# A hybrid decoder layer on one core: subtractions and convolution taps moved from VectorE to GpSimd and ScalarE, and other weight buffers in one stage

## The chip, the core and the metric

The kernel runs on one core of a Trainium2 chip. A core has TensorE (PE, matrix products out of SBUF into PSUM), VectorE (DVE), ScalarE (ACT), GpSimd (POOL) and SyncE (SP, which issues most DMA transfers). Each engine works through its own queue in order, and waits on semaphores for the others. SBUF has 128 partitions; a "128x512" operation works on 512 elements in each. The metric is the device time of one execution in microseconds (us), lower is better. The granted TensorE clock of a stretch is given as a share of full speed.

## What is computed

One decoder layer, for 512 tokens of width 2048 in fp32. One input projection feeds two branches, whose gated outputs are summed, projected and added to the input (the reference, cut):

```python
h = rms_norm(x, norm_g)
proj = jnp.einsum('bsd,dn->bsn', h, w_in)
(q_a, k_a, v_a, o_a, i_a, f_a, z_a, c_q, c_kv, k_r, z_b, g_a, g_b) = jnp.split(proj, offsets, axis=-1)

qk_a = jax.nn.silu(causal_depthwise_conv(jnp.concatenate([q_a, k_a], axis=-1), conv_w))
q_a, k_a = jnp.split(qk_a, 2, axis=-1)
h_a = mlstm_chunkwise(q_a, k_a, v_a, i_a + gate_bias[:H_A], f_a + gate_bias[H_A:])
h_a = rms_norm(h_a, mlstm_norm_g)
y_a = jnp.einsum('bsc,cd->bsd', jax.nn.sigmoid(o_a) * h_a * jax.nn.silu(z_a), w_a)
...
o_b = causal_attention(q_b, k_b, v_b)
y_b = jnp.einsum('bsc,cd->bsd', o_b * jax.nn.silu(z_b), w_b)

y = jax.nn.sigmoid(g_a) * y_a + jax.nn.sigmoid(g_b) * y_b
return x + jnp.einsum('bsd,de->bse', y, w_out)
```

The convolution has four taps along the tokens, for each channel by itself:

```python
xp = jnp.pad(x, ((0, 0), (CONV_K - 1, 0), (0, 0)))
out = xp[:, CONV_K - 1:] * w[CONV_K - 1]
for j in range(CONV_K - 1):
    out = out + xp[:, j:j + s_len] * w[j]
```

## The kernel before

**Numbers in two parts.** Each fp32 operand of a product is split into a high and a low part: ACT casts it (`split`, L105), DVE subtracts the cast from the source (L106). A product is then three matmuls, high by high, high by low and low by high (`mm3`, L113 to L115, and in the Strassen stage L506 to L508).

**Stages.** The order of the work on each engine comes from a scheduler in the tile framework, which keeps data and buffer dependencies; the code gives the rough order by `weave` (a main generator, with a filler put between its steps) and by `later` (a list of small pieces, one of which `run_later` takes after each step of a product).

1. To about 124 us: the input is transposed and normalized, and the latents and gates are projected (`load_c`, `proj_tok`). Beside it, `build(j)` makes for each of eight pairs of row blocks the operands of the Strassen products: `normal` (L304) scales `f` by the norm, `parts` splits it, `combine` (L323 to L326) makes four sums of 256 elements, `split_sums` splits these.
2. To about 905 us: ten jobs of a one-level Strassen scheme (`strassen`). A job makes 1024 columns of the input projection with seven products p = 0 to 6 in place of eight, and each product has four steps j, 28 steps of 12 matmuls in a job. `prep` loads a block of weights (`rx`, 5 buffers, and `rr`, a ring of 8) and, for p = 1, 2, 4 and 6, subtracts blocks (`minus`, L462). `part` splits the result into `wh` (3 buffers) and `wl` (2 buffers). `mult` multiplies. `finish` takes the results out of PSUM. In the code `prep` runs two steps ahead of `mult`, `part` one step.
3. To about 1387 us: eight pairs of attention heads (`pair_attn`), with the projections for later pairs as filler. The outputs `go` are stored to `gb` (L857) by SP.
4. To about 1690 us: the mLSTM branch. `conv_qk` projects two blocks of 128 channels of q or k, takes each through the convolution and silu, and splits it into `qkT`. In `evac` ACT copies the projection from PSUM into `xp`, behind three zeros (L969, L970); DVE multiplies by the last tap (L980) and adds the other three taps one by one (L977). ACT's tanh (L985) and three more operations make silu and the split. `pair_qk` of the next two heads, and then the first block of `out_b`, are the filler for `heads`. There, POOL makes the causal mask of each tile (`affine_select`, L1037) and the reciprocal root for the norm (`rsqrt`, L120 to L124).
5. To the end: `out_b(1..3)`, the product with `w_a`, and the one with `w_out`.

**Weights of stages 3 to 5.** `load_w` takes 256 KB at a time: `raw` from SP (4 buffers, L137), `whi` (NB_W = 3 buffers) and `wlo` (NB_L = 2). All come from one pool, `wp`, from the attention on to the end. `reload` in stage 4 brings back the attention's outputs and splits them into `g`; it takes nothing but `raw` from that pool. `out_b(d)` also loads `u`, 1 MB of gates.

**The pools.** `open_pool` and `close_pool` give and take space of SBUF. A tile of a pool that is opened in the place of a closed one waits for the tiles that lay there.

Of the kernel before, what the change touches and what calls it, by code (L numbers as in the profile page):

```python
# [19 lines left out]
P = 128  # L20
# [17 lines left out]
NB_X, NB_RING, NB_HI, NB_LO = 5, 8, 3, 2  # L38

# [5 lines left out]
def hybrid_kernel(  # L45
# [81 lines left out]
    wpool = [None]  # L127

    def load_w(src, col, width, kn, first=0):
        per = max(1, 512 // width)  # L130
        hi = lo = None
        for i in range(kn):
            k = (i + first) % kn
            if k % per == 0:
# [6 lines left out]
                hi = wp.tile([P, per, width], F32R, tag="whi", name=nm("whi"), bufs=NB_W)  # L141
                lo = wp.tile([P, per, width], F32R, tag="wlo", name=nm("wlo"), bufs=NB_L)
# [157 lines left out]
    def build(j):  # L300
        f = whole[j]

        def normal():
            V.tensor_tensor(f, f, rB.unsqueeze(1).broadcast_to([P, 2, S]), ALU.mult)  # L304
# [15 lines left out]
        def combine():  # L320
            a, b = tmp(512, "s12"), tmp(512, "s34")
            s1, s2, s3, s4 = a[:, 0:256], a[:, 256:512], b[:, 0:256], b[:, 256:512]
            V.tensor_tensor(s1, f[:, 0, 256:512], f[:, 1, 256:512], ALU.add)  # L323
            V.tensor_tensor(s3, f[:, 0, 0:256], f[:, 0, 256:512], ALU.subtract)
            V.tensor_tensor(s2, s1, f[:, 0, 0:256], ALU.subtract)
            V.tensor_tensor(s4, f[:, 1, 0:256], s2, ALU.subtract)  # L326
            sums.extend((a, b))
# [112 lines left out]
    def strassen(jobs, comb):  # L440
# [15 lines left out]
        def prep(c, p, j):  # L456
# [4 lines left out]
            def minus(dst, a, b):  # L461
                V.tensor_tensor(dst, a, b, ALU.subtract)  # L462
# [497 lines left out]
    close_pool("bpa")  # L960
    big_pool[:] = [(open_pool("bph"), NB_HEAD)]


    def conv_qk(p, base, blk, res):

        def evac(s, ps):
            k = blk + 2 * p + s
            xp = tmp(516, "xp")
            G.memset(xp[:, 0:3], 0.0)  # L969
            A.copy(xp[:, 3:515], ps)  # L970
            o = big([P, 2, S], F32R, "qkT")
            cv = tmp(512, "cv")
            th = tmp(512, "th")

            def taps(j0, j1):
                for j in range(j0, j1):
                    V.scalar_tensor_tensor(cv, xp[:, j:j + S], cw[:, k, j:j + 1], cv, ALU.mult, ALU.add)  # L977
# [273 lines left out]
```

## Time and profile before

| | |
|---|---|
| runs | 2171.72, 2172.4 and 3008.73 us, median 2172.4 us |
| profiled execution | 2176.62 us, of it 2174.9 us in the span of the profile |
| granted TensorE clock, mean | 0.991 |
| busy: PE, DVE, ACT, POOL | 2121.5, 1395.4, 983.0, 173.2 us |

"Busy" is the time in which an engine executes; a matmul is shown from its start to its modelled end, and overlaps the next. A row of a group of instructions reads: line of the code, engine, operation, output <- inputs by the names in the code (numbers left out), partitions x elements, count; then busy us in total, mean ns of one, and the idle time of the engine just before them, with what ended it. A row of the timeline begins with start and duration in us.

### The profile page before, as it was taken

How to read it: one execution, taken by the hardware profiler on the slowest of the kernel's cores; microseconds unless marked ns; L12 is line 12 of the kernel's file. 1: busy time of each engine (PE TensorE's matmuls, PEld its weight loads, DVE VectorE, ACT ScalarE, POOL GpSimd, SP SyncE). 2: the span in 40 equal slices, each digit the busy share in tenths (PEclk: the TensorE clock that was granted, in tenths of full speed). 3: DMA queues.
4: the chain of work that ended last, by engine and by line, in shares of the span. 5: the costliest groups of instructions: out<-in, count | busy, mean ns of one | idle time of the engine just before them, and what ended most of it. 6: DMA issues, size and time to landing. Idle time of an engine off the chain costs nothing. (4 is left out here: it accounts for less than half of the span.)

```text
span 2174.9 us, 28907 instructions
## 1 busy us (share of the span) xinstructions
PE 2121.5 (98%) x10200; PEld 1787.8 (82%) x10200; DVE 1395.4 (64%) x2260; ACT 983.0 (45%) x2025; POOL 173.2 (8%) x306
## 2 busy tenths in 40 slices
PE   8999999999999999899999999999989999999999
PEld 8878888888888888688888888877867888888889
DVE  5877788887778788656666677766565334444333
ACT  7544444444444544445555556454445223222221
POOL 0000000000000000222222222011111000000000
PEclk9999999999999999999999999999999999999999
DMA  6645424633642462632222222464544425332443
GB/s 171 166 166 184 149 90 149 184 108 105 185 149 90 149 204 92 215 89 75 83 77 80 81 80 73 155 190 144 159 134 157 136 97 160 126 131 92 136 131 117
DMA packets 205314, 286.02 MB, mean 132 GB/s; under 512 B 31216, under 2 KB 111472, under 8 KB 204144
## 3 DMA queue, kind: packets, MB, share of 16 engines
q1 hardware_dynamic: 189040, 256.90, 38.9%
q10 hardware_dynamic: 16128, 27.27, 3.6%
q8 instruction: 80, 1.31, 0.3%
q14 instruction: 66, 0.54, 0.1%
HBM read 240.07 MB, written 44.04 MB: 131 GB/s over the span
## 5 line engine op out<-in xcount | busy, mean ns | idle before, releaser
L106 DVE TENSOR_TENSOR wlo<-raw,whi 128x512 fp32r<-128x512 f32 (+3 forms) x432 | 284.3, 661 | 383.5 <-PE acc L114 252.3
L105 ACT CAST whi<-raw 128x512 fp32r<-128x512 f32 (+3 forms) x432 | 259.1, 600 | 526.8 <-PE acc L115 338.0
L106 DVE TENSOR_TENSOR wl<-rx,wh 128x1024 fp32r<-128x1024 f32 x160 | 196.5, 1228 | 114.7 <-PE aux L507 64.7
L105 ACT CAST wh<-rx 128x1024 fp32r<-128x1024 f32 x160 | 168.9, 1055 | 177.9 <-PE acc L508 109.0
L113 PE MATMUL acc<-whi,g 128*128 128x512 f32 x512 | 201.5, 396 | 5.9 <-ACT g L105 5.9
L115 PE MATMUL acc<-whi,g 128*128 128x512 f32 x512 | 199.7, 393 | 1.8 <-DVE g L106 1.8
L114 PE MATMUL acc<-wlo,g 128*128 128x512 f32 x512 | 200.6, 392 | 0.0
L105 ACT CAST wh<-rr 128x1024 fp32r<-128x1024 f32 x120 | 126.4, 1053 | 160.7 <-PE aux L508 88.1
L106 DVE TENSOR_TENSOR wl<-rr,wh 128x1024 fp32r<-128x1024 f32 x120 | 146.3, 1219 | 27.6 <-PE aux L507 14.6
L506 PE MATMUL acc<-wh,sh 128*128 128x512 f32 x400 | 155.6, 389 | 0.0
L507 PE MATMUL acc<-wl,sh 128*128 128x512 f32 x400 | 155.6, 389 | 0.0
L508 PE MATMUL acc<-wh,sl 128*128 128x512 f32 x400 | 155.6, 389 | 0.0
L113 PEld LDWEIGHTS acc<-whi,g 128*128 128x128 f32 x512 | 96.8, 189 | 25.7 <-ACT g L105 6.5
L115 PEld LDWEIGHTS acc<-whi,g 128*128 128x128 f32 x512 | 96.9, 190 | 22.2 <-DVE g L106 2.2
L114 PEld LDWEIGHTS acc<-wlo,g 128*128 128x128 f32 x512 | 96.9, 189 | 20.3 <-DVE wlo L106 0.8
L115 PE MATMUL acc<-h8h,wlo 128*128 128x512 f32 x256 | 102.8, 406 | 10.3 <-DVE wlo L106 10.3
L113 PE MATMUL acc<-whi,y 128*128 128x512 f32 (+1 forms) x320 | 111.1, 348 | 0.0
L115 PE MATMUL acc<-whi,y 128*128 128x512 f32 (+1 forms) x320 | 111.0, 347 | 0.0
L114 PE MATMUL acc<-wlo,y 128*128 128x512 f32 (+1 forms) x320 | 111.0, 347 | 0.0
L113 PE MATMUL acc<-h8h,whi 128*128 128x512 f32 x256 | 103.6, 405 | 2.3 <-ACT whi L105 2.3
L114 PE MATMUL acc<-h8l,whi 128*128 128x512 f32 x256 | 102.5, 400 | 0.0
L113 PE MATMUL acc<-ht,whi 128*128 128x512 f32 x256 | 101.2, 395 | 0.0
(357 smaller groups left out, 5052.6 us busy)
## 6 DMA issues: line engine op xcount, KB each, us to landing
rr<-in_w_in SPq DMA_DIRECT2D x120, 512.0 KB, 4.6
raw<-in_w_in SPq DMA_DIRECT2D x128, 256.0 KB, 2.8
rx<-in_w_in SPq DMA_DIRECT2D x40, 512.0 KB, 5.0
raw<-in_w_b SPq DMA_DIRECT2D x64, 256.0 KB, 3.1
raw<-in_w_a SPq DMA_DIRECT2D x64, 256.0 KB, 3.2
raw<-in_w_out SPq DMA_DIRECT2D x64, 256.0 KB, 3.0
raw<-in_w_ukv SPq DMA_DIRECT2D x32, 256.0 KB, 2.8
raw<-in_w_uq SPq DMA_DIRECT2D x32, 192.0 KB, 2.4
```

The source lines that it names most:

```text
L105: A.copy(dst_hi, src)
L106: V.tensor_tensor(dst_lo, src, f32(dst_hi), ALU.subtract)
L113: PE.matmul(ps, lh, rh, start=start, stop=False)
L114: PE.matmul(ps, lh, rl, start=False, stop=False)
L115: PE.matmul(ps, ll, rh, start=False, stop=stop)
L506: PE.matmul(out[i], lh[:, tok], hi[:, n, :], start=first, stop=False, skip_group_check=cont)
L507: PE.matmul(out[i], lh[:, tok], lo[:, n, :], start=False, stop=False, skip_group_check=cont)
L508: PE.matmul(out[i], ll[:, tok], hi[:, n, :], start=False, stop=k == H8 - 1, skip_group_check=cont)
```

## The change

`normal` and `combine` in `build`, and `minus` in `prep`, are issued to GpSimd (`G`) in place of VectorE (`V`). In `conv_qk`, ACT takes the projection out of PSUM four times, each time scaled by one tap, and GpSimd adds three of these copies, shifted by 1, 2 and 3 tokens, to the fourth; `xp` and its zeros are gone. After the attention the pool `wp` is closed and `wph` opened, with six buffers for `whi` and six for `wlo`; after the mLSTM stage `wph` is closed and `wp` opened again with three and two. The pool of `u` is now two pools, `up0` (for `out_b(0)`) and `up1`.

```diff
 NB_X, NB_RING, NB_HI, NB_LO = 5, 8, 3, 2
+NB_W2, NB_L2 = 6, 6
...
-    wpool = [None]
+    wpool = [None, NB_W, NB_L]
...
-                hi = wp.tile([P, per, width], F32R, tag="whi", name=nm("whi"), bufs=NB_W)
-                lo = wp.tile([P, per, width], F32R, tag="wlo", name=nm("wlo"), bufs=NB_L)
+                hi = wp.tile([P, per, width], F32R, tag="whi", name=nm("whi"), bufs=wpool[1])
+                lo = wp.tile([P, per, width], F32R, tag="wlo", name=nm("wlo"), bufs=wpool[2])
...
         def normal():
-            V.tensor_tensor(f, f, rB.unsqueeze(1).broadcast_to([P, 2, S]), ALU.mult)
+            G.tensor_tensor(f, f, rB.unsqueeze(1).broadcast_to([P, 2, S]), ALU.mult)
...
-            V.tensor_tensor(s1, f[:, 0, 256:512], f[:, 1, 256:512], ALU.add)
-            V.tensor_tensor(s3, f[:, 0, 0:256], f[:, 0, 256:512], ALU.subtract)
-            V.tensor_tensor(s2, s1, f[:, 0, 0:256], ALU.subtract)
-            V.tensor_tensor(s4, f[:, 1, 0:256], s2, ALU.subtract)
+            G.tensor_tensor(s1, f[:, 0, 256:512], f[:, 1, 256:512], ALU.add)
+            G.tensor_tensor(s3, f[:, 0, 0:256], f[:, 0, 256:512], ALU.subtract)
+            G.tensor_tensor(s2, s1, f[:, 0, 0:256], ALU.subtract)
+            G.tensor_tensor(s4, f[:, 1, 0:256], s2, ALU.subtract)
...
             def minus(dst, a, b):
-                V.tensor_tensor(dst, a, b, ALU.subtract)
+                G.tensor_tensor(dst, a, b, ALU.subtract)
...
     close_pool("bpb")
     close_pool("bpa")
+    close_pool("wp")
+    wpool[:] = open_pool("wph"), NB_W2, NB_L2
     big_pool[:] = [(open_pool("bph"), NB_HEAD)]
...
-            xp = tmp(516, "xp")
-            G.memset(xp[:, 0:3], 0.0)
-            A.copy(xp[:, 3:515], ps)
+            cv = tmp(512, "cv")
+            A.activation(cv, ps, AF.Copy, scale=cw[:, k, 3:4])
+            for d in range(1, 4):
+                th = tmp(512, "th")
+                A.activation(th, ps, AF.Copy, scale=cw[:, k, 3 - d:4 - d])
+                G.tensor_tensor(cv[:, d:], cv[:, d:], th[:, :S - d], ALU.add)
             o = big([P, 2, S], F32R, "qkT")
...
-            def taps(j0, j1):
-                for j in range(j0, j1):
-                    V.scalar_tensor_tensor(cv, xp[:, j:j + S], cw[:, k, j:j + 1], cv, ALU.mult, ALU.add)
...
-                V.tensor_scalar(cv, xp[:, 3:515], cw[:, k, 3:4], None, ALU.mult)
...
-            later.extend((first, second, third, fourth))
+            later.extend((lambda: None, silu, lambda: split(o[:, 0, :], o[:, 1, :], cv)))
...
     drain(filler)
     close_pool("bph")
+    close_pool("wph")
+    wpool[:] = open_pool("wp"), NB_W, NB_L
     g2p = open_pool("g2p")
+    ups.append(open_pool("up1", "right"))
```

**The products' stage, first job.** DVE before, from the first subtractions of product 1 on. `rx` and `rr` are blocks of weights, the number tells one buffer's tile from another, `wl` is a low part, and the rows of L106 are splits:

```order
L462 TENSOR_TENSOR rx_1606<-rr_1670,rx_1606 128x1024
L106 TENSOR_TENSOR wl_1674<-rx_1646,wh_1673 128x1024
L462 TENSOR_TENSOR rx_1608<-rr_1695,rx_1608 128x1024
L462 TENSOR_TENSOR rx_1614<-rr_1715,rx_1614 128x1024
L106 TENSOR_TENSOR wl_1699<-rx_1606,wh_1698 128x1024
L462 TENSOR_TENSOR rx_1646<-rr_1737,rx_1646 128x1024
L106 TENSOR_TENSOR wl_1719<-rx_1608,wh_1718 128x1024
L462 TENSOR_TENSOR rx_1606<-rr_1757,rx_1606 128x1024
L462 TENSOR_TENSOR rx_1608<-rr_1776,rx_1608 128x1024
L106 TENSOR_TENSOR wl_1741<-rx_1614,wh_1740 128x1024
```

POOL in the changed kernel, the subtractions of the same job (line 463 now), from the last sum over the input (L327) on:

```order
L327 TENSOR_TENSOR s_321_1665<-hn_347,s_320_1664 128x256
L463 TENSOR_TENSOR rx_1606<-rr_1670,rx_1606 128x1024
L463 TENSOR_TENSOR rx_1608<-rr_1695,rx_1608 128x1024
L463 TENSOR_TENSOR rx_1614<-rr_1715,rx_1614 128x1024
L463 TENSOR_TENSOR rx_1646<-rr_1737,rx_1646 128x1024
L463 TENSOR_TENSOR rx_1606<-rr_1757,rx_1606 128x1024
L463 TENSOR_TENSOR rx_1608<-rr_1776,rx_1608 128x1024
L463 TENSOR_TENSOR rx_1614<-rr_1796,rx_1614 128x1024
L463 TENSOR_TENSOR rx_1646<-rr_1818,rx_1646 128x1024
L463 TENSOR_TENSOR rr_1757<-rr_1757,rr_1670 128x1024
L463 TENSOR_TENSOR rr_1776<-rr_1776,rr_1695 128x1024
L463 TENSOR_TENSOR rx_1606<-rx_1606,rr_1982 128x1024
```

Before, the subtractions stood between the splits on one queue. Now they stand one behind the other on POOL, product 6 (`rx<-rx,rr`) mixed with product 4 (`rr<-rr,rr`), and DVE has the splits alone.

**From the attention to the mLSTM stage, SP.** The stores of `go` and the loads of weights; `raw` from `in_w_in`, 128x2x256, are the weights of `conv_qk(0)`. Before:

```order
L137 DMA raw_12102<-in_w_ukv 128x512
L137 DMA raw_12120<-in_w_ukv 128x512
L137 DMA raw_12595<-in_w_in 128x2x256
L137 DMA raw_12613<-in_w_in 128x2x256
L137 DMA raw_12631<-in_w_in 128x2x256
L137 DMA raw_12649<-in_w_in 128x2x256
L137 DMA raw_12667<-in_w_in 128x2x256
L137 DMA raw_12685<-in_w_in 128x2x256
L857 DMA gb_7332<-go_12240 128x512
L137 DMA raw_12703<-in_w_in 128x2x256
```

In the changed kernel:

```order
L138 DMA raw_12120<-in_w_ukv 128x512
L858 DMA gb_7332<-go_12240 128x512
L858 DMA gb_7332<-go_12316 128x512
L858 DMA gb_7333<-go_12509 128x512
L1109 DMA u_14945<-ggb_1580 128x2048
L858 DMA gb_7333<-go_12585 128x512
L138 DMA raw_12599<-in_w_in 128x2x256
L138 DMA raw_12617<-in_w_in 128x2x256
L138 DMA raw_12635<-in_w_in 128x2x256
```

The weights of `conv_qk(0)` stood ahead of the last four stores; now they stand behind all of them, and behind the load of `u`.

**The same place on PE.** `ptb` and `vl` belong to the last tile of the attention, `acc` of `whi` and `h8h` to `conv_qk(0)`. Before, in the middle of the last pair of heads:

```order
L811 MATMUL aux_12166<-krl_11862,qst_11860 128x256
L835 MATMUL aux_12203<-ident,pr_12097 128x128 x4
L113 MATMUL acc_12593<-h8h_827,whi_12597 128x512
L114 MATMUL acc_12593<-h8l_828,whi_12597 128x512
L115 MATMUL acc_12593<-h8h_827,wlo_12598 128x512
L113 MATMUL acc_12594<-h8h_827,whi_12597 128x512
L114 MATMUL acc_12594<-h8l_828,whi_12597 128x512
```

In the changed kernel, at the end of that pair:

```order
L115 MATMUL aux_12572<-ptb_12514,vh_12040 128x256
L116 MATMUL aux_12572<-ptb_12514,vl_12041 128x256
L114 MATMUL acc_12597<-h8h_827,whi_12601 128x512
L115 MATMUL acc_12597<-h8l_828,whi_12601 128x512
L116 MATMUL acc_12597<-h8h_827,wlo_12602 128x512
```

The projection of `conv_qk(0)` stood between the tiles of the last pair; now its first matmul stands behind the last one of the attention.

More of the change, by code (lines that the diff above doesn't have):

```diff
@@ L967, in evac, with silu @@
             k = blk + 2 * p + s
-            xp = tmp(516, "xp")
-            G.memset(xp[:, 0:3], 0.0)
-            A.copy(xp[:, 3:515], ps)
-            o = big([P, 2, S], F32R, "qkT")
-            cv = tmp(512, "cv")
-            th = tmp(512, "th")
-            def taps(j0, j1):
-                for j in range(j0, j1):
-                    V.scalar_tensor_tensor(cv, xp[:, j:j + S], cw[:, k, j:j + 1], cv, ALU.mult, ALU.add)
-            def first():
-                V.tensor_scalar(cv, xp[:, 3:515], cw[:, k, 3:4], None, ALU.mult)
-                taps(0, 1)
-            def second():
-                taps(1, 3)
+            cv = tmp(512, "cv")
[4 more added lines that the diff above has]
+                G.tensor_tensor(cv[:, d:], cv[:, d:], th[:, :S - d], ALU.add)
+            o = big([P, 2, S], F32R, "qkT")
+            def silu():
+                th = tmp(512, "th")
                 A.activation(th, cv, AF.Tanh, scale=0.5)
-            def third():
                 V.scalar_tensor_tensor(cv, th, 1.0, cv, ALU.add, ALU.mult)
-                A.copy(o[:, 0, :], cv)
-            def fourth():
-                V.tensor_tensor(o[:, 1, :], cv, f32(o[:, 0, :]), ALU.subtract)
-            later.extend((first, second, third, fourth))
+            later.extend((lambda: None, silu, lambda: split(o[:, 0, :], o[:, 1, :], cv)))
             res.append(o)
@@ L1113, in lazily @@
         return get
-    u_t = []
+    u_t, ups = [], []
     def out_b(d):
-        u = up.tile([P, T, 512], F32, tag=f"u{d}", name=f"u{d}")
+        u = ups[-1].tile([P, T, 512], F32, tag=f"u{d}", name=f"u{d}")
         SP.dma_start(u, gb_g[d])
@@ L1160, in hybrid_kernel @@
                 gp = open_pool("gp", "right")
-                up = open_pool("up", "right")
+                ups.append(open_pool("up0", "right"))
                 gB = []
@@ L1210, in hybrid_kernel @@
         drain(proj_tok(load_w(w_out, c0, width, KD), width, get_y, KD, evac_out))
-    for name in ("g2p", "wp", "up", "gp"):
+    for name in ("g2p", "wp", "up1", "up0", "gp"):
         close_pool(name)
```

## The prediction

> **What bounds the kernel now.** I read the busy times of the whole span first (TensorE, PE below, is busy 98% of 2174.9 us), then the same by stage, then what PE waited for, then single steps in order of time. The stages, with the busy time of each engine (in brackets the number of instructions), the granted TensorE clock, the share of DMA time and GB/s:
>
> ```profile
> core 0: us, PE busy (x) PEld busy (x) DVE busy (x) ACT busy (x) POOL busy (x), PEclk, DMA share, GB/s
> 0.00:124.20 124.20, 109.68 (x648) 104.78 (x648) 88.12 (x188) 80.02 (x261) 4.55 (x18) 1.00 0.66 172
> 124.20:904.97 780.77, 773.89 (x3388) 637.97 (x3389) 617.41 (x646) 369.71 (x429) 13.07 (x24) 0.99 0.47 144
> ...
> 1336.00:1387.00 51.00, 48.07 (x265) 39.17 (x264) 39.28 (x108) 27.11 (x80) 12.51 (x18) 1.00 0.22 64
> 1387.00:1500.00 113.00, 105.93 (x496) 86.50 (x495) 73.98 (x138) 53.09 (x124) 11.94 (x42) 0.98 0.60 190
> 1500.00:1600.00 100.00, 92.16 (x441) 75.85 (x440) 62.78 (x130) 51.72 (x134) 14.85 (x48) 0.93 0.48 145
> 1600.00:1650.00 50.00, 41.96 (x191) 34.51 (x190) 28.87 (x61) 24.57 (x60) 5.07 (x16) 0.90 0.49 158
> 1650.00:1700.00 50.00, 47.95 (x234) 39.69 (x234) 24.60 (x51) 21.73 (x51) 5.29 (x14) 1.00 0.53 175
> ```
>
> Row two is the stage of the seven products. PE misses only 6.9 us of 780.8 there, so whatever leaves DVE (VectorE) in that stage can win at most this; what matters is whether a slower maker of operands can make PE wait. Rows four to seven, the mLSTM stage, have 25.0 us of PE idle (7.1 + 7.8 + 8.0 + 2.1) and a lower clock: 0.02 x 113 + 0.07 x 100 + 0.10 x 50 = 14 us. That is all the change can gain by its conv part. The profile's total of 2176.62 us is the time in which I make the sum; it lies 4.2 us over the median of the runs, 2172.4.
>
> **Part 1: 160 subtractions of the products move to GpSimd (POOL).** Groups of instructions, with busy us, mean ns, and idle time before:
>
> ```profile
> L462 DVE TENSOR_TENSOR rx<-rr,rx 128x1024 f32<-128x1024 f32 x80 | 97.5, 1223 | 2.0
> L462 DVE TENSOR_TENSOR rx<-rx,rr 128x1024 f32<-128x1024 f32 x40 | 48.2, 1217 | 0.0
> L462 DVE TENSOR_TENSOR rr<-rr,rr 128x1024 f32<-128x1024 f32 x40 | 47.9, 1219 | 0.3
> L106 DVE TENSOR_TENSOR wl<-rx,wh 128x1024 fp32r<-128x1024 f32 x160 | 196.5, 1228 | 114.7 <-PE aux L507 64.7 <-PE acc L507 47.6 <-PE aux L508 1.8
> L757 POOL TENSOR_TENSOR qro<-qro,qrt 128x512 f32<-128x512 f32 x8 | 10.7, 1332 | 0.1
> L756 POOL TENSOR_TENSOR qrt<-qr,rq 128x256 f32<-128x256 f32 x8 | 5.9, 735 | 0.0
> L760 POOL TENSOR_TENSOR kn<-kn,rs 128x1024 f32<-128x1024 f32 x8 | 15.2, 1898 | 0.0
> ```
>
> DVE loses 193.6 us. The price on POOL of 1024 elements with two full operands is not in the trace. Of the eight operations of 512 elements (1332 ns in the mean) one took 1627 ns behind a DVE operation (937.15 in the next lines); the other seven then took (8 x 1332 - 1627) / 7 = 1290. From 256 to 512 elements the price grows by 1290 - 735 = 555 ns, and two steps more give 1290 + 2 x 555 = 2.40 us. The lower bound is the 1.90 us of the 1024-element row, whose second operand is broadcast; the upper is twice the 512 group, 2.66. I take 2.40, as the rows of two full operands are nearest. By duration alone this is hidden: 16 x 2.40 = 38 us in a job of 28 steps (the steps are timed below).
>
> But POOL and DVE hinder each other. Start, duration and engine of single instructions, from the attention stage and from the end of the products:
>
> ```profile
> 937.15 1.63 POOL L757 TENSOR_TENSOR qro<-qro,qrt 128x512 f32<-128x512 f32 x1
> ...
> 881.65 0.60 POOL L644 TENSOR_TENSOR rq<-rope,gqr 128x128 f32<-128x128 f32 x1
> ...
> 881.86 1.47 DVE L106 TENSOR_TENSOR wl<-rx,wh 128x1024 fp32r<-128x1024 f32 x1
> ...
> 882.22 1.43 POOL L643 TENSOR_TENSOR rk<-rope,gkr 128x128 f32<-128x128 f32 x1
> ...
> 883.39 0.50 PE L507 MATMUL aux<-wl,h8h 128*128 128x512 f32 x1 [3.47 <-DVE wl L106]
> ...
> 883.61 0.51 POOL L644 TENSOR_TENSOR rk<-rope,gkr 128x128 f32<-128x128 f32 x1
> ...
> 884.20 1.26 POOL L659 TENSOR_TENSOR krope<-rk 128x256 f32<-128x256 f32 x1
> ...
> 884.79 1.75 DVE L106 TENSOR_TENSOR wl<-rx,wh 128x1024 fp32r<-128x1024 f32 x1
> ...
> 1348.02 1.90 POOL L760 TENSOR_TENSOR kn<-kn,rs 128x1024 f32<-128x1024 f32 x1
> ...
> 1348.26 1.67 DVE L817 TENSOR_TENSOR nmx<-nmx,srq 128x1 f32<-128x1 f32 x1
> ```
>
> A split (wl) that takes 1.23 us in the mean took 1.47 and 1.75 here, and ended at 883.33 and 886.54: both times 1.08 us after the POOL operation that ran when it was issued had ended (882.25, 885.46). An operation on one element, nmx, took 1.67 us, and ended with POOL's kn (1349.93 and 1349.92). In the other direction the POOL operation at 882.22 took 1.43, where its like takes 0.51, and ended 0.32 us after the split. So a DVE operation with two operands in SBUF and a POOL operation that reads SBUF do not run side by side: the later one waits, and from the other's end it still needs 1.08 us (a split) or all but 0.19 us of its own time (POOL). At 883.39 PE has waited 3.47 us for that split.
>
> So where a subtraction and a split alternate, one turn takes 1.08 + (2.40 - 0.19) = 3.29 us. PE needs for a step:
>
> ```profile
> 418.72 0.39 PE L506 MATMUL acc<-wh,h8h 128*128 128x512 f32 x1
> ...
> 418.75 1.22 DVE L106 TENSOR_TENSOR wl<-rx,wh 128x1024 fp32r<-128x1024 f32 x1 [1.55 <-PE acc L507]
> ...
> 421.44 0.39 PE L506 MATMUL aux<-wh,h8h 128*128 128x512 f32 x1
> ...
> 421.67 0.39 PE L507 MATMUL aux<-wl,h8h 128*128 128x512 f32 x1
> ```
>
> A step starts at 418.72 and the next at 421.44, 2.72 us later. The split in between ends at 419.97 and is first used at 421.67, so a split can be 1.70 late (with two wl buffers DVE cannot be further ahead). Each turn then falls 3.29 - 2.72 = 0.57 us behind. In a job the subtractions come in two rows of eight (products 1 and 2; products 4 and 6, which the order on POOL puts into one row). Eight turns fall 4.56 us behind, of which 1.70 are covered: 2.86 us, twice in a job, ten jobs: **57 us**. At 1.90 us on POOL a turn is 2.79, and eight turns stay within the cover: 0. At 2.66 a turn is 3.55: 2 x 10 x (8 x 0.83 - 1.70) = 99 us. Bounds 0 and 99; a gain beyond the 6.9 us of idle PE is excluded.
>
> The Trainium skill (GPSIMD Engine Reference, section 3.1) gives 4497 ns for an fp32 tensor_tensor of 2048 elements on GpSimd against 2293 on VectorE, and its section 4.1 says to keep elementwise work on VectorE, which speaks against this change. Half of 4497, an estimate, is 2.25 us; the sum by it would be 2 x 10 x (8 x 0.42 - 1.70) = 33 us in place of 57. No run here shows this size, and the rows of two full operands lie above it.
>
> **Part 2: sums over the input (normal, combine) on POOL.** Eight products with a broadcast operand, 1.90 us each by the row of kn, and 32 of 256 elements at 0.74: 39 us on a queue that is busy 4.6 us in the first 124 us (row one). They run beside the loads of the first stage; DVE is busy 88 us there, so few can be shifted by POOL's turns. I take 2 us, between 0 and 10 (10 if the last sums are late for product 1 by a row of eight chains).
>
> **Part 3: the pools between attention and mLSTM.** Closing `wp` and opening `wph` puts every weight load and split of conv_qk(0) behind the end of the attention, as the order above shows. Before, the q half of conv_qk(0) fills PE's gaps there. Groups within 1336 to 1387 us, and a load's time to landing:
>
> ```profile
> L113 PE MATMUL acc<-h8h,whi 128*128 128x512 f32 x16 | 6.8, 424 | 0.0
> ...
> L113 PE MATMUL acc<-ht,whi 128*128 128x512 f32 x16 | 6.4, 402 | 0.0
> ...
> L106 DVE TENSOR_TENSOR wlo<-raw,whi 128x512 fp32r<-128x512 f32 x8 | 5.5, 685 | 0.6 <-issue 0.3 <-PE acc L115 0.3
> ...
> raw<-in_w_in SPq DMA_DIRECT2D x128, 256.0 KB, 2.8
> ```
>
> That is 32 groups of three matmuls, twelve of which make a step of 2.72 us: 32 x 3 x 0.227 = 21.8 us of the 48.1. Without it the tail has 26.3 us of PE work, but DVE has 39.3 - 5.5 = 33.8 us and each step waits for the one before; I take 39 us of the 51, between 34 and 45. Then the queue of SP has the stores of go and a load of 1 MB ahead of the first weights: 2.8 us for a load, 0.6 for the cast, 0.7 for the last product on DVE and its store's issue, 5 to 8 us with the load ahead; I take 6. Then the 21.8 us come. Sum 39 + 6 + 21.8 - 51 = **16 us**; bounds 34 + 5 + 21.8 - 51 = 10 and 45 + 8 + 21.8 - 51 = 24. The second change of pools, ahead of out_b(1), I cost at nothing: its loads follow in the same order as before, behind out_b(0), whose matmuls cover them. Without that cover it would be the same 5 to 8 us.
>
> **Part 4: convolution and buffers.** What PE waits for between 1387 and 1700 us (total, times, longest), and two groups:
>
> ```profile
> PE acc L115 <- DVE wlo L106: 10.1, 6, 2.1
> PE acc L113 <- ACT g L105: 5.9, 2, 4.6
> PE aux L113 <- DVE wda L1042: 2.5, 4, 0.8
> PE acc L113 <- ACT whi L105: 2.3, 1, 2.3
> ...
> L977 DVE SCALAR_TENSOR_TENSOR cv<-xp,cw,cv 128x512 f32<-128x512 f32 x48 | 35.9, 749 | 0.5
> ...
> L1081 ACT ACTIVATE go<-aux,mgh 128x512 f32<-128x512 f32 x16 | 10.1, 681 | 5.5 <-PE aux L1079 5.4
> ```
>
> DVE loses 35.9 us and the 16 first taps, POOL gets 48 additions at 1.29 = 62 us, ACT 48 scaled copies at 0.68 = 33 us more, on an engine busy 45 to 52% there. With six buffers a split can be five weights ahead, where two low halves allowed one. The waits for wlo and whi, 12.4 us, are what this can remove; I take 10. The clock that follows such waits costs 14 us; I take 5 of them. The waits for g and wda stay: reload uses no weight buffer. Against it, POOL's additions now stand ahead of its affine_select and rsqrt, which the heads wait for, and hinder the splits on DVE: 2 us. Sum **-13 us**; bounds -22 (12.4 and two thirds of 14) and -3 (the additions give most of it back).
>
> The Trainium skill (TensorE: Matmul & The Clock Gate, part 1) lets the clock fall after an idle window of about 3.4 us. By it only the wait of 4.6 us would cost clock, the 5 us would not come, and the sum would be -8. The trace differs: the clock is below 1.00 in three stretches, with one wait of that length.
>
> **Sum:** 57 + 2 + 16 - 13 = 62; 2176.6 + 62 = 2238.6, and less the 4.2 us between this execution and the median: **2234 us**, slower by 2.8%.
>
> **Rivals.** (a) *The turns stay covered.* If POOL takes about 2.0 us, or the rows of eight are broken by loads, the products lose 0 to 8: 2172 + 5 + 2 + 16 - 13 = 2182, range 2172 to 2200. For it speaks the row of 1.90; against it the slope of the two-operand rows. (b) *Not slower, the gain decides.* Turns covered, and the attention's tail, freed of splits and filler, ends in 34 us while the first loads land under it: 34 + 1 + 21.8 - 51 = 6; with the full gain of 22, 2172 + 2 + 6 - 22 = 2158. It decides once POOL is below 2.0 us and the gap at the pools below 2 us. Against it: the store and the load stand one behind the other on SP. (c) *The stalls cost clock.* If each row of eight makes PE idle enough for one stretch at half rate as in the mLSTM stage (0.07 x 100 us over three or four waits there, some 1.7 us each), 20 x 1.7 = 34 us come on top: 2268, and 2285 with 2.5 us on POOL. Against it: a stall of 0.57 us is much shorter than the waits there. (d) *The buffers do not do what they say*: the four raw buffers stay, so the splits get no further ahead than loads land, and part 4 is -3: 2244, within the forecast's range.
>
> **How the numbers follow.** Chances: forecast (with d) 0.62, own range 2205 to 2262; (a) 0.18; (b) 0.04; (c) 0.16. About 2% is what a measurement of this kernel can tell from no change, here 2216 and 2129 us. Of the forecast's 0.62 some 0.10 lies below 2216, so within 2%: 0.18 + 0.03 + 0.10 = 0.31; slower 0.52 + 0.16 = 0.68; faster 0.01. From 2178 to 2285 leaves out (b), a third of (a) and the top of (c): 0.04 + 0.06 + 0.07 = 0.17, and 0.02 of the forecast.
>
> **What would show it.** The group of 160 subtractions on POOL near 2.4 us alone and longer in turns; the wl splits on DVE above 1.23 in the mean, up to 3.4 each; waits of PE at L507 for wl in steps of product 1, 2, 4, 6 of every job, some 57 us in the stage; the tail of the attention without acc matmuls, and a wait of 5 to 8 us ahead of the first whi; fewer waits for wlo behind it, and a clock nearer 1.00. The prediction is wrong if POOL's subtraction is below 2.1 us, if wl does not lengthen beside it, or if PE has acc matmuls before the attention's end.

## The result, and the profile after

The changed kernel takes 2335.4 us in the median of four runs (2332.6 to 2338.4), the kernel before 2174.3, now with one run more. One of its four runs took 3008.73 us, and the ratio leaves it out: 1.0745, with a 95% interval from 1.0723 to 1.0768. The change makes the kernel slower by 7.5%, where 2.8% was forecast and 2285 us was the upper end of the range. The profiled execution took 2332.55 us, 2330.8 of it in the span, 155.9 more than before.

The same instruction can be looked up in both traces. The table gives the start of a matmul in each (from its first or last start, as the trace lists them), and so the place at which the time is lost:

| matmul | before, us | after, us | later by | gained since the row above |
|---|---|---|---|---|
| first of the products (acc<-wh,a) | 124.2 | 151.7 | 27.5 | 27.5 |
| first transpose of k in the attention (aux<-ident,kn) | 969.6 | 1076.4 | 106.8 | 79.3 |
| last of the attention (aux<-ptb,vh) | 1385.4 | 1495.6 | 110.2 | 3.4 |
| first scores of the mLSTM heads (aux<-qkT,qkT) | 1414.9 | 1558.3 | 143.4 | 33.2 |
| first of w_out (acc<-whi,y) | 1992.5 | 2148.3 | 155.8 | 12.4 |

Every stretch between two of these marks has become longer. The stretches of the changed kernel that answer to those shown of before, with the same columns:

```profile
core 0: us, PE busy (x) PEld busy (x) DVE busy (x) ACT busy (x) POOL busy (x), PEclk, DMA share, GB/s
0.00:151.70 151.70, 117.45 (x648) 111.01 (x648) 101.33 (x153) 80.89 (x265) 55.56 (x58) 0.93 0.56 144
151.70:1011.80 860.10, 811.54 (x3391) 633.81 (x3392) 691.33 (x482) 367.55 (x428) 496.11 (x184) 0.99 0.41 131
1011.80:1443.20 431.40, 431.06 (x2258) 372.51 (x2257) 285.25 (x676) 231.88 (x688) 105.25 (x127) 1.00 0.29 84
1443.20:1496.20 53.00, 35.14 (x172) 27.97 (x170) 34.14 (x100) 22.77 (x72) 12.40 (x17) 0.82 0.04 16
1496.20:1526.20 30.00, 24.11 (x97) 19.46 (x96) 9.69 (x14) 8.19 (x14) 0.00 (x0) 0.87 0.60 185
1526.20:1856.30 330.10, 288.67 (x1356) 239.81 (x1355) 177.80 (x311) 176.97 (x412) 92.58 (x152) 0.94 0.46 146
```

In the products' stage (row two) DVE is *busier* than before, 691 us in place of 617, although 160 instructions have left it: it is now counted busy while it waits for POOL. PE has 48.6 us of idle time there instead of 6.9. That is 42 of the 79 us by which the stage has grown; the rest is counted as busy. A matmul is shown for 0.39 us, while in an undisturbed step the next one starts 0.23 us after it, so up to 0.16 us of every wait, and shorter gaps altogether, lie inside a busy time. Row four is the end of the attention without its filler: 53 us, not shorter than the 51 before, with 18 us of idle PE and a clock of 0.82. The groups of the products' stage show the price of an operation and of the turn:

```profile
L107 DVE TENSOR_TENSOR wl<-rx,wh 128x1024 fp32r<-128x1024 f32 x160 | 312.4, 1974 | 108.1 <-PE acc L508 54.9
L463 POOL TENSOR_TENSOR rx<-rr,rx 128x1024 f32<-128x1024 f32 x80 | 244.1, 3074 | 228.7 <-DVE wl L107 213.6
L107 DVE TENSOR_TENSOR wl<-rr,wh 128x1024 fp32r<-128x1024 f32 x120 | 271.1, 2277 | 21.5 <-PE aux L508 15.0
```

What PE waits for there, as total, times and longest:

```profile
PE acc L508 <- DVE wl L107: 35.9, 63, 3.1
PE aux L508 <- DVE wl L107: 11.3, 21, 3.5
```

The splits that took 1.23 us now take 1.97 and 2.28 in the mean. The subtractions on POOL take 3.07 in the mean; the shortest of the 160 took 2.36, near the 2.40 of the prediction. PE waits for the splits, as forecast.

**The start.** POOL, ACT and DVE of the changed kernel around 66 to 72 us of the span:

```profile
65.40 1.16 POOL L326 TENSOR_TENSOR s<-s,hn 128x256 f32<-128x256 f32 x1
66.53 2.52 POOL L305 TENSOR_TENSOR hn<-hn,rB 128x1024 f32<-128x1024 f32 x1
69.01 1.02 POOL L327 TENSOR_TENSOR s<-hn,s 128x256 f32<-128x256 f32 x1
...
70.06 1.14 ACT L106 CAST sh<-s 128x512 fp32r<-128x512 f32 x2 [5.09 <-POOL s L327]
71.11 0.49 ACT L106 CAST whi<-raw 128x368 fp32r<-128x368 f32 x1
...
66.77 2.67 DVE L107 TENSOR_TENSOR wlo<-raw,whi 128x368 fp32r<-128x368 f32 x1
```

Between the third and the fourth sum of one block, the order on POOL has the scaling (hn) of another, 2.52 us. ACT waits 5.09 us for the fourth sum, and the cast of the next weights (whi, 71.11) stands behind the cast of the sums in ACT's queue. On DVE a split of 368 elements lasts 2.67 us and ends at 69.44, 0.39 us after hn. Up to 151.7 us PE waits 20.8 us for wlo, 2.9 before.

**After the attention.** The last matmul, the first load and the first matmul behind it:

```profile
1496.08 0.41 PE L116 MATMUL aux<-ptb,vl 128*128 128x256 f32 x1
1496.53 0.69 DVE L857 TENSOR_TENSOR go<-aux,gz 128x512 f32<-128x512 f32 x1 [3.08 <-PE aux L116]
1497.25 0.32 SPq L858 DMA_DIRECT2D gb<-go  x1
1497.61 5.83 SPq L138 DMA_DIRECT2D raw<-in_w_in  x5
1501.71 0.62 ACT L106 CAST whi<-raw 128x512 fp32r<-128x512 f32 x1 [8.72 <-DMA raw<-in_w_in]
1502.38 0.79 PE L114 MATMUL acc<-h8h,whi 128*128 128x512 f32 x1 [5.89 <-ACT whi L106]
```

The product go and its store come first, then the loads (issued from 1497.61 on), the cast, and PE 5.89 us after its last work.

**The mLSTM stage.** What PE waits for most from 1533 to 1850 us (total, times, longest):

```profile
PE aux L114 <- ACT qkT L106: 14.7, 4, 4.2
PE aux L114 <- DVE wda L1032: 13.4, 4, 4.0
PE acc L114 <- ACT g L106: 6.1, 1, 6.1
```

The waits for wlo and whi are gone, as forecast. In their place stand waits for the convolution's result (qkT) and for the heads' decay tile (wda), 28 us in all.

### The profile page after: what moved, and what is told of

Its sections match the earlier page's. It is cut to its first block, busy times and chain, and to the rows that moved or that the text cites. A ratio compares the mean times of both kernels' runs of the same rounds, so it can differ in the third digit from the quotient of the medians.

```text
span 2330.8 us, 29111 instructions
## 1 busy us (share of the span) xinstructions
PE 2178.8 (93%) x10200; PEld 1801.8 (77%) x10200; DVE 1473.6 (63%) x1996; ACT 1009.9 (43%) x2073; POOL 761.9 (33%) x538
## 5 line engine op out<-in xcount | busy, mean ns | idle before, releaser
L107 DVE TENSOR_TENSOR wlo<-raw,whi 128x512 fp32r<-128x512 f32 (+3 forms) x432 | 297.1, 691 | 413.5 <-PE acc L115 278.1
L106 ACT CAST whi<-raw 128x512 fp32r<-128x512 f32 (+3 forms) x432 | 258.3, 600 | 529.4 <-PE acc L116 344.9
L107 DVE TENSOR_TENSOR wl<-rx,wh 128x1024 fp32r<-128x1024 f32 x160 | 312.4, 1974 | 108.1 <-PE acc L508 54.9
L463 POOL TENSOR_TENSOR rx<-rr,rx 128x1024 f32<-128x1024 f32 x80 | 244.1, 3074 | 228.7 <-DVE wl L107 213.6
L107 DVE TENSOR_TENSOR wl<-rr,wh 128x1024 fp32r<-128x1024 f32 x120 | 271.1, 2277 | 21.5 <-PE aux L508 15.0
L106 ACT CAST wh<-rx 128x1024 fp32r<-128x1024 f32 x160 | 168.2, 1052 | 189.4 <-PE acc L509 97.9
L106 ACT CAST wh<-rr 128x1024 fp32r<-128x1024 f32 x120 | 125.5, 1051 | 193.2 <-PE aux L509 92.9
L508 PE MATMUL acc<-wl,sh 128*128 128x512 f32 x400 | 165.2, 413 | 29.5 <-DVE wl L107 29.3
L463 POOL TENSOR_TENSOR rr<-rr,rr 128x1024 f32<-128x1024 f32 x40 | 115.6, 2889 | 91.2 <-DVE wl L107 91.2
L508 PEld LDWEIGHTS acc<-wl,sh 128*128 128x128 f32 x400 | 75.4, 189 | 74.3 <-DVE wl L107 60.7
L463 POOL TENSOR_TENSOR rx<-rx,rr 128x1024 f32<-128x1024 f32 x40 | 124.9, 3122 | 16.5 <-DMA rr<-in_w_in 16.0
L116 PEld LDWEIGHTS acc<-whi,g 128*128 128x128 f32 x512 | 96.6, 189 | 20.2
```

Source lines behind the costliest of these rows:

```text
L106: A.copy(dst_hi, src)
L107: V.tensor_tensor(dst_lo, src, f32(dst_hi), ALU.subtract)
L116: PE.matmul(ps, ll, rh, start=False, stop=stop)
L463: G.tensor_tensor(dst, a, b, ALU.subtract)
L508: PE.matmul(out[i], lh[:, tok], lo[:, n, :], start=False, stop=False, skip_group_check=cont)
```

## The experiments

Each starts from the kernel before, if nothing else is said. The second of two times is the median of runs of the kernel before that stood beside the experiment on the same chip.

### The four parts, each alone

The subtractions alone:

```diff
             def minus(dst, a, b):
-                V.tensor_tensor(dst, a, b, ALU.subtract)
+                G.tensor_tensor(dst, a, b, ALU.subtract)
```

> The kernel before with one edit: the 160 subtractions of the products on GpSimd. Theory (a split on VectorE and a subtraction on GpSimd exclude each other, a turn is 2.4 + 1.0 = 3.4 us against the step's 2.72): the products' stage grows by about 79 us, as between 124 and 911 us in the changed kernel, and nothing else moves: 2174 + 79 = 2253 us. The subtraction takes 2.4 us alone and 3.3 to 3.4 in turns; the wl splits 2.0 to 2.3 us in the mean. Rival (the sums over the input, which come late in the changed kernel, carry part of these 79 us into the products): 30 to 60 us, the rest comes only together with the sums.

2259.1 us against 2177.7: ratio 1.0369 (1.0354 to 1.0385), 81 us. The whole loss of the products' stage, 79 us in the table, comes with this edit alone; the late sums carry nothing into it that could be seen. Two of POOL's turns in a row of subtractions of products 4 and 6:

```profile
513.98 3.38 POOL L462 TENSOR_TENSOR rr<-rr,rr 128x1024 f32<-128x1024 f32 x1
517.32 3.38 POOL L462 TENSOR_TENSOR rx<-rx,rr 128x1024 f32<-128x1024 f32 x1
```

One turn from start to start is 3.34 us, 3.29 in the prediction, against PE's step of 2.72: each turn falls 0.62 us behind.

The starts of the products on PE show where these 81 us lie (a product takes 10.88 us when nothing waits). Six of the ten jobs lose 2.4 us in products 0 to 2, and six lose 3.4 in products 3 and 4, where POOL has its second row; products 5 and 6 lose nothing. That is 5.8 us in a job, close to the 2 x 2.86 of the prediction, and 58 us in ten. The rest, 24 us, lies in single jobs. Products 3 and 4 lose 7.0 to 8.2 us in place of 3.4 in jobs 2, 3, 8 and 9 (numbers from 0), 16 us more in all. Products 0 to 2 of the first job lose 4 us more than 2.4, beyond what the kernel before loses there, and those of jobs 3, 4 and 9 together 3 us more, for a reason that is not shown. In jobs 2 and 3 the results go through silu on DVE (ot<-ot,co), in jobs 8 and 9 they are split (ol<-co,oh), and in the first job DVE works out the gates of the mLSTM branch (lg_e). All of these have two operands in SBUF:

```profile
L428 DVE SCALAR_TENSOR_TENSOR ot<-ot,co 128x512 f32<-128x512 f32 x12 | 15.0, 1263 | 0.0
L519 DVE TENSOR_TENSOR co<-acc,s 128x512 f32<-128x512 f32 x20 | 13.6, 678 | 0.0
L106 DVE TENSOR_TENSOR ol<-co,oh 128x512 fp32r<-128x512 f32 x12 | 12.6, 1049 | 1.2 <-ACT oh L105 1.2
L906 DVE SCALAR_TENSOR_TENSOR lg_e<-lg_e,lg_w 128x32 f32<-128x32 f32 x7 | 7.7, 1099 | 0.2
```

Before, the first took 683 ns, the third 684 and the fourth 187. They take turns with POOL as the splits do, and the splits stand behind them. The second row has one operand in PSUM (acc); it took 680 ns before and takes 678 here, though it too stands beside subtractions on POOL.

The sums over the input alone (`normal` and `combine` on `G`):

> The kernel before with one edit: normal and combine on GpSimd. Theory (the splits of the first stage on VectorE take turns with GpSimd, and ACT's cast of the next weights stands behind a cast that waits for a sum): PE waits for wlo 20 us more between 64 and 85 us of the span, the first product starts at 152 instead of 124 us: 2174 + 27 = 2201 us. Rival (the start only shifts because the subtractions of the first job wait behind these sums on GpSimd): under 10 us, 2184.

2203.7 against 2177.7: ratio 1.0121 (1.0106 to 1.0136), 26 us. The waits for wlo are 19.3 us up to the first products, as in the changed kernel, and the time is lost without any subtraction on POOL, so the late start needs no help from them.

Of these, `combine` alone on `G`, `normal` on `V`:

> The kernel before with the four sums of combine alone on GpSimd, normal on VectorE. Theory (the start is late because ACT's cast of the sums, and behind it the next weights' cast, waits for a chain of sums that take turns with splits): most of the 26 us stay, 15 us or more: 2192 us. Rival (the 2.6 us operations of normal hold VectorE and the chain up): 8 us or less, 2184 us.

2189.2 against 2174.9: ratio 1.0064 (1.0043 to 1.0085), 14 us, between the two expectations. Waits for wlo fall to 8.1 us. So the chain of sums makes a good half of the 26 us (9 to 18 us, by the interval), and the scaling between them the rest; the run does not separate how much of each is POOL's turn with DVE and how much ACT's queue.

The pools alone (cut; the buffers and the two pools of `u` as in the change):

```diff
...
+    close_pool("wp")
+    wpool[:] = open_pool("wph"), NB_W2, NB_L2
     big_pool[:] = [(open_pool("bph"), NB_HEAD)]
...
     close_pool("bph")
+    close_pool("wph")
+    wpool[:] = open_pool("wp"), NB_W, NB_L
```

> The kernel before with the pools of the changed one: wp closed after the attention, wph with six buffers of each half, then wp again; convolution and subtractions as before. Theory (the projection of conv_qk(0) leaves the attention's last 50 us, which do not get shorter without it, and its first weights are loaded only then): 31 us later at the boundary, and the six buffers take the waits for wlo (10 us) and part of the clock (5 us) away: 2174 + 31 - 15 = 2190 us. Rival (the six buffers are worth nothing, since the waits for wlo come from a VectorE busy with the taps): 2174 + 31 - 2 = 2203 us, waits for wlo still 8 us or more in the mLSTM stage.

2196.1 against 2177.7: ratio 1.0086 (1.0068 to 1.0104), 18 us. PE still waits 6.4 us for the first whi, and no wait for wlo is listed behind it. The six buffers remove the waits that they were meant to remove; the gap that makes room for them costs more.

The convolution alone (`evac` of the changed kernel, pools as before):

> The kernel before with the convolution of the changed one (four scaled copies on ACT, three additions on GpSimd), pools as before. Theory (the chain from a projection to its heads gets longer: the additions of 1.1 to 1.4 us stand one behind another on GpSimd, and PE waits for qkT and wda): 14.7 + 11 us of new waits, less the 10 us for wlo that a relieved VectorE removes: 2174 + 16 = 2190 us. Rival (the waits for qkT come from the pools, because the filler of two heads runs out earlier): no waits for qkT, 2174 - 10 = 2164 us.

2199.9 against 2177.7: ratio 1.0107 (1.0092 to 1.0122), 22 us. More than the 16 expected, and by another way: the waits for wlo did not go, they doubled to 19.9 us in the stage, beside 6.5 for wda and 4.6 for qkT. DVE lost the taps, but between 1390 and 1720 us the 78 splits of weights take 0.77 us in the mean, where those of before took 0.69, and 32 operations on the heads' outputs (og<-num,rsn,og), which stand in the same queue, 1.12 in place of 0.48. How much of the waits each of them makes is not shown.

The four alone add up to 81.4 + 26.0 + 18.5 + 22.3 = 148 us of the 161 lost.

### Exclusion, or an operand that comes late?

A stream of subtractions on POOL that depends on no DVE work and that nobody waits for, and the same with memsets (cut; `extra` is a tile in the place of the fifth rx buffer):

```diff
...
             def minus(dst, a, b):
                 V.tensor_tensor(dst, a, b, ALU.subtract)
+                if c["job"] and j % 2:
+                    G.tensor_tensor(extra, f32(sh[0]), f32(sl[0]), ALU.subtract)
```

> The kernel before, its subtractions on VectorE as they were, and 72 subtractions of 1024 elements more on GpSimd, of two tiles that lie in SBUF through the whole stage, into a tile that nothing reads (the fifth rx buffer goes for it). GpSimd waits for nothing and nothing waits for GpSimd. Theory (exclusion): every one of them takes a turn with a VectorE operation of two SBUF operands, 72 turns of 3.3 us in which VectorE does 1.6 jobs' work instead of 3.1: about 110 us more, 2285 us; splits near the stream of 2 to 3.4 us. Rival (the loss in the changed kernel is that of an operand that comes late from a slower, in-order queue): 2178 us, as nothing depends on the stream.

2310.9 against 2176.5: ratio 1.0623 (1.0584 to 1.0661), 134 us, more than the 110 expected.

> The same with 144 memsets of 1024 elements on GpSimd in place of the 72 subtractions, about as long in all and without a read of SBUF. Theory (it is the two reads of SBUF that exclude each other): no loss beside that of the fifth rx buffer, 2175 to 2190 us, splits at 1.23 us. Rival (any work on GpSimd slows VectorE): as long as with the subtractions.

2173.4 against 2176.5: ratio 0.9986 (0.9976 to 0.9996). The groups of the first and then of the second:

```profile
L465 POOL TENSOR_TENSOR extra<-sh,sl 128x1024 f32<-128x1024 f32 x72 | 218.4, 3033 | 45.3 <-PE acc L115 39.7
L106 DVE TENSOR_TENSOR wl<-rx,wh 128x1024 fp32r<-128x1024 f32 x160 | 217.4, 1360 | 108.5 <-PE aux L510 63.3 <-PE acc L510 45.2
```

```profile
L106 DVE TENSOR_TENSOR wl<-rx,wh 128x1024 fp32r<-128x1024 f32 x160 | 196.5, 1228 | 112.7 <-PE aux L511 65.9 <-PE acc L511 46.8
...
L466 POOL MEMSET extra<- 128x1024 f32 x144 | 137.6, 955 | 49.0 <-ACT sh L105 40.8
```

The means are taken over all ten jobs, the stream of subtractions ends in the first. Beside it, single operations of DVE look like this:

```profile
168.49 3.36 DVE L106 TENSOR_TENSOR wl<-rx,wh 128x1024 fp32r<-128x1024 f32 x1
171.77 2.34 DVE L902 TENSOR_SCALAR lg_z<-lg_e 128x32 f32<-128x32 f32 x1
```

72 useless subtractions, the last of which starts at 320.7 us of the span, cost 134 us: the first product starts 23 us late, its job takes 107 us longer, and the jobs behind it lose nothing. From 147 to 330 us the granted clock was 0.75, so part of the 134 us is clock that falls with the waits. 144 memsets, which run from 101 to 247 us, cost nothing and leave the 43 splits between 130 and 246 us at 1.22 us. So POOL's reads alone, without an operand that comes late, hold up DVE and through it PE. The Trainium skill (SBUF — State Buffer, "Who interferes with whom") says the same: a DVE instruction with two SBUF inputs contends with a GpSimd instruction that reads SBUF, not with one that only writes it. These two runs agree with it. In the changed kernel operands do come late too, but seldom: ACT's casts (wh) wait for POOL's subtractions 20.2 us in all, 13 times, and PE waits for such a cast twice only, 5.6 us ahead of the first product and 0.3 once behind it.

### Does each subtraction cost the same?

Every second subtraction on POOL:

```diff
-                V.tensor_tensor(dst, a, b, ALU.subtract)
+                (G if j % 2 else V).tensor_tensor(dst, a, b, ALU.subtract)
```

> The kernel before with every second subtraction (j = 1 and 3) on GpSimd, 80 in all. Theory: in two steps (5.44 us of PE) the turns need 2 x 1.08 for splits, 1.22 for the subtraction on VectorE and 2.2 for the one on GpSimd, 5.6 us: almost covered, so 0 to 12 us more, 2178 to 2190 us; the splits' mean between 1.5 and 1.9 us. Rival (a subtraction on GpSimd costs PE the same 0.5 us wherever it stands): half of the 81 us, 2218 us.

2237.8 against 2176.5: ratio 1.0292 (1.0275 to 1.0309), 61 us. Both expectations were wrong: the half costs three quarters of the whole.

Those of product 6 alone:

```diff
             elif p == 6:
-                minus(x[j], x[j], ring[2, j])
+                G.tensor_tensor(x[j], x[j], ring[2, j], ALU.subtract)
```

> The kernel before with the 40 subtractions of product 6 alone on GpSimd; they are wanted two products after they can be made. Theory (what a subtraction on GpSimd costs depends on where its turns fall: these four take turns with splits of products 4 and 5, which are ahead by 1.7 us, and no operand of the next steps waits for them): 4 turns of 0.62 less 1.7, 0.8 us in a job, 2176 + 8 = 2184 us at most. Rival (each one costs PE the same, 0.5 to 0.75 us, as the 81 us for 160 and the 61 us for 80 would have it): 2196 to 2206 us.

2234.6 against 2174.9: ratio 1.028 (1.0263 to 1.0297), 60 us, for a quarter of the subtractions. A cover of 1.70 us, with which the expectation reckons, does not help here. What it had missed is in the trace of the kernel before. DVE in one job (job 2), from product 3's splits to product 4's:

```profile
312.35 0.68 DVE L528 TENSOR_TENSOR s<-aux,s 128x512 f32<-128x512 f32 x1
312.95 1.21 DVE L106 TENSOR_TENSOR wl<-rr,wh 128x1024 fp32r<-128x1024 f32 x1
314.09 0.68 DVE L528 TENSOR_TENSOR s<-aux,s 128x512 f32<-128x512 f32 x1
314.69 1.21 DVE L462 TENSOR_TENSOR rr<-rr,rr 128x1024 f32<-128x1024 f32 x1
...
324.94 0.68 DVE L519 TENSOR_TENSOR co<-acc,s 128x512 f32<-128x512 f32 x1
325.55 1.21 DVE L462 TENSOR_TENSOR rx<-rx,rr 128x1024 f32<-128x1024 f32 x1
```

Each row starts when the one before ends, for 14 us: both subtractions and the products' results (s, co) stand there, and DVE has no idle time. In the run with product 6 on POOL, DVE and then POOL at the same place:

```profile
328.35 3.31 DVE L462 TENSOR_TENSOR rr<-rr,rr 128x1024 f32<-128x1024 f32 x1
331.59 3.38 DVE L106 TENSOR_TENSOR wl<-rr,wh 128x1024 fp32r<-128x1024 f32 x1
335.00 1.23 DVE L462 TENSOR_TENSOR rr<-rr,rr 128x1024 f32<-128x1024 f32 x1
336.15 3.41 DVE L106 TENSOR_TENSOR wl<-rr,wh 128x1024 fp32r<-128x1024 f32 x1
```

```profile
327.52 3.07 POOL L477 TENSOR_TENSOR rx<-rx,rr 128x1024 f32<-128x1024 f32 x1 [67.19 <-DMA rr<-in_w_in]
331.30 2.59 POOL L477 TENSOR_TENSOR rx<-rx,rr 128x1024 f32<-128x1024 f32 x1 [0.71 <-DMA rr<-in_w_in]
```

A subtraction that took DVE some 1.13 us (the spacing of rows above) now takes DVE 2.2 us of waiting: four of them, 4 to 5 us, in a stretch without reserve. By the starts of the products in both traces, PE lost 4.8 to 6.0 us in each job, all of it in products 3 and 4. With all 160 on POOL, product 4's subtractions have left DVE as well, and these two products lost only 3.4 us in six of the jobs. That fits the prices: the 40 alone cost 60 us, and the other 120 only 22 more.

If so, the same 40 operations must cost less in a stretch in which DVE has reserve. Written into `ring[2, j]`, they have to wait for product 5's split and fall into products 5 and 6:

```diff
-                minus(x[j], x[j], ring[2, j])
+                G.tensor_tensor(ring[2, j], x[j], ring[2, j], ALU.subtract)
...
-            w = c["ring"][1 if p in (3, 4) else 2, j] if p in (3, 4, 5) else c["x"][j]
+            w = c["ring"][1 if p in (3, 4) else 2, j] if p in (3, 4, 5, 6) else c["x"][j]
```

> As the run with product 6's 40 subtractions on GpSimd, but written into ring[2, j] in place of x[j], so that each has to wait for product 5's split of that block and falls beside the splits of products 5 and 6. Theory (VectorE has no idle time from product 3's splits to product 4's, so 2.27 us of exclusion in place of 1.13 lengthens that stretch; it has idle time in products 5 and 6): little is left, 0 to 1 us in a job, 2175 to 2187 us, and no waits in products 3 and 4. Rival (a subtraction on GpSimd costs 1.1 to 1.5 us of PE wherever it stands): 2220 to 2235 us.

> The same edit with the 40 subtractions on VectorE: the control for what the later time and the ring slots cost by themselves. Theory: 2172 to 2180 us, as before. Rival (the later release of the ring delays the next job's loads): 2185 us or more, and then the run on GpSimd is to be read against this one.

2203.0 us on POOL and 2180.8 on VectorE, against 2177.5: ratios 1.0124 (1.0107 to 1.0141) and 1.0019 (1.0006 to 1.0033). The place decides more than half of the price, 25 us in place of 60, and nothing is lost any more in products 3 and 4. But the expected 0 to 10 was too low, 22 us over the control: product 5 loses 1.4 to 1.5 us in six of the jobs, 2.7 to 4.9 in jobs 2, 3, 8 and 9. DVE in the late run, in job 2, shows what was left out of the sum:

```profile
339.04 3.15 DVE L519 TENSOR_TENSOR co<-s,s 128x512 f32<-128x512 f32 x2
342.11 1.21 DVE L106 TENSOR_TENSOR wl<-rr,wh 128x1024 fp32r<-128x1024 f32 x1
343.25 3.48 DVE L428 SCALAR_TENSOR_TENSOR ot<-ot,co 128x512 f32<-128x512 f32 x2
```

The results of the products (co<-s,s and ot<-ot,co) have two operands in SBUF as well. Two of them take 3.15 and 3.48 us where one alone takes 0.68, and the splits stand behind them in DVE's queue.

### Buffers without the gap, and the convolution on top

A second pool beside `wp`, opened after the first half of conv_qk(0), with the weights' tiles alternating between both, three and three high ones, two and four low ones (cut; the low ones are shown):

```diff
+                more, turn = wpool[1], wpool[2] % 6
+                wpool[2] += 1
...
+                if more is None or turn < NB_L:
                     lo = wp.tile([P, per, width], F32R, tag="wlo", name=nm("wlo"), bufs=NB_L)
+                else:
+                    lo = more.tile([P, per, width], F32R, tag="wlo", name=nm("wlo"), bufs=4)
...
         yield from conv_qk(p, OFF_QA, 0, qs)
+        wpool[1] = wpx
```

> The kernel before with six whi and six wlo buffers in the mLSTM stage, but without closing wp: a second pool is opened beside it after the first half of conv_qk(0), and the tiles alternate between both (u again in two pools). Theory (the buffers took 15 us off in the run with the pools alone, and the 31 us came from the closed pool): 2176 - 15 = 2161 us, attention's tail filled as before, no waits for wlo in the mLSTM stage. Rival (the 15 us were only the convolution catching up what the gap had held back): 2170 to 2178 us.

2159.7 against 2175.2: ratio 0.9928 (0.9914 to 0.9942), 15.5 us faster than before and the fastest of all the kernels here. No wait for wlo is left in the stage, and the filler stays in the attention. Both effects of the pools are so shown apart: 15.5 us less by the buffers, and the difference to the pools alone, 18.5 + 15.5 = 34 us, for the place where they were opened.

On top of it, the convolution of the changed kernel, with its additions on POOL and then on VectorE:

> The kernel with the second pool, and the convolution of the changed kernel. Theory (the convolution costs the same with buffers, by GpSimd's turns with VectorE and by the longer chain): 2161 + 22 to 32 = 2183 to 2193 us; waits for qkT and wda of 25 us or so, none for wlo. Rival (with enough buffers the convolution's relief of VectorE pays): 2155 us or less.

> As the run with second pool and changed convolution, but its 48 additions on VectorE in place of GpSimd; the scaled copies stay on ACT. Theory (the loss comes from the additions on GpSimd, not from ACT's copies): within 8 us of the kernel with the second pool alone, 2161 to 2169 us. Rival (four copies on ACT hold the accumulators and delay the casts): 15 us or more above it.

2197.9 us (ratio to before 1.011, 1.0089 to 1.0131) and 2174.6 (0.9996, 0.9987 to 1.0006). With the second pool the convolution costs 38 us, not 22 to 32. Read the other way, the buffers gain 15.5 us beside the old convolution and nothing beside the new one: 22.7 us over the kernel before with them, 22.3 without. 23 of the 38 us belong to the additions on POOL. The other 15 stay with the additions on VectorE. That is what the rival had for the four scaled copies on ACT, but the changed `evac` also cuts its work into other pieces, and no run takes the two apart; nor is it shown how much of the 23 is turns with DVE and how much the longer chain. What PE waits for most in the first of the two:

```profile
PE aux L113 <- ACT qkT L105: 14.7, 4, 4.2
PE aux L113 <- DVE wda L1038: 14.6, 4, 4.0
```

These are the two largest waits of the changed kernel's mLSTM stage. With 81.4 + 26.0 + 18.5 + 38.2 = 164 us the parts now make up its loss of 161 within 3 us.

## Why the prediction was wrong

The sign was right, and so was the mechanism of the largest term. The sum of 62 us fell 99 short of the 161 measured, and each of its four terms came out too low: by 24 us for the subtractions, 24 for the sums over the input, 16 to 18 for the pools, and 36 for convolution and buffers.

- **Subtractions, 57 forecast, 81 measured.** The 2.40 us, the exclusion and the turn (3.29, measured 3.34) hold, and the row of eight comes out in most jobs: 2.4 and 3.4 us where the prediction has 2.86 twice. The step that failed is to take this "twice in a job, ten jobs", with the splits as the only operations of DVE that take turns with POOL. DVE has others with two operands in SBUF, and where they fall beside subtractions on POOL the rows get longer: 16 us in four jobs, 4 in the first. All of them are in the trace of before. That the term came within a third was partly luck as well: the same cover, used for product 6 alone, gave 8 us and 60 were measured, since DVE had no idle time in that stretch. The prediction had read the cover from one step with idle time in it (the split at 418.75).
- **The price from the Trainium skill.** Half of the 4497 ns that the Trainium skill (GPSIMD Engine Reference, section 3.1) gives for 2048 elements is an estimate of 2.25 us; the shortest of the 160 took 2.36. The sum by this estimate, 33 us, would have been further off.
- **Sums over the input, 2 forecast (0 to 10), 26 measured.** Three parts failed. "So few can be shifted by POOL's turns" went by the mean, 88 of 124 us; in the 30 us from 60 to 90, in which nearly all the scaling and three of the eight chains of sums are made, DVE was busy 27. The price of `normal` was taken from kn, 1.90, and is 2.39 at the least and 2.65 in the mean. And nobody was named who waits behind: ACT's casts of the weights stand behind the cast of the sums.
- **The pools, 16 forecast, 32 to 34 measured** (2 for the tail, 5.9 for the gap and 24 for the work behind it; 34 between the two runs). The gap was right: 6 us, measured 5.9. "I take 39 us of the 51" failed: the tail of the attention took 53. The sum took PE's 26 us of work and DVE's 34 as the floor and added 5 for steps that wait for one another; but these waits filled the whole stretch, and the filler had cost next to no time in them. Its 21.8 us came back in full, as 24 at a clock of 0.87.
- **Convolution and buffers, -13 forecast; buffers -15, convolution +38.** The waits for wlo went as said. What failed is "hinder the splits on DVE: 2 us": the chain from projection to qkT now runs through three additions on POOL of 1.28 us each in the mean, one after another, and through ACT twice; two channels' blocks stand in one queue, and the heads' wda waits too. The additions on POOL made 23 us of the 38; what the other 15 are made of stays open. (By its own rows ACT is busy 43 to 52% of the stage, not 45 to 52; nothing hangs on it.)
- **The clock.** The rival of lost clock was given 34 us on top, in the products. The granted clock fell from 0.991 to 0.976 in the mean, which is, as an estimate, 0.024 x 2331 less 0.009 x 2175, 36 us and so about that size. But the products stay at 0.99; it falls where PE has longer waits, 0.93 at the start, 0.82 and 0.87 around the end of the attention. The Trainium skill (TensorE: Matmul & The Clock Gate, part 1) names an idle window of about 3.4 us for the fall; in the attention's tail the clock was 0.82 with no wait above 3.3 us, and in the kernel before 0.93 from 1500 to 1600 us with none above 2.1. So here it was lower beside shorter waits too; at which share of idle time it falls, no run shows.

## What to carry to other kernels

In this kernel VectorE and GpSimd were one resource for operations that read two operands from SBUF on the one and subtractions on the other: moving a subtraction from 1.1 us of that resource to 2.3 made a full stretch longer, however idle GpSimd looked. So look for the densest stretch of VectorE and not for its mean, and count every operation with two operands in SBUF there, not only those that the change is about. Before a filler is moved away, ask whether the work around it gets shorter without it; where it was a chain, as in the attention's tail here, the filler was almost free. And give new buffers a place that waits for nothing: the same six buffers cost 18 us behind a closed pool and gained 15 beside an open one.

## What the hardware showed that was not expected

- On POOL a broadcast operand was cheap only in one form: kn<-kn,rs of 1024 elements took 1.90 us, hn<-hn,rB of the same size, with an operand repeated over its two halves, 2.39 at the least, as much as two full operands (2.36).
- POOL's memsets of 1024 elements (955 ns) left the splits beside them at 1.22 us, while in the kernel before even an operation of one element on DVE (nmx) was held for the whole of POOL's kn.
- One operand in SBUF was not always safe. Two operations of 128x32 elements with one (TENSOR_SCALAR) took 0.18 us in the kernel before; lg_z<-lg_e took 2.34 beside the subtractions, and lg_w<-gt 0.86 beside the memsets. An operation with one operand in SBUF and one in PSUM (co<-acc,s) was not held, 0.68 us in the mean with all subtractions on POOL and without.
- TensorE's clock fell to 0.82 over 53 us in which PE was busy 35 us and never waited longer than 3.3 us at a time.
